# Two gated feed-forward layers: first groups of the second product at even distances, first tiles' taps and SiLU one per step, last roundings and plain products in another order

## The chip, the core and the metric

The kernel runs on one core of a Trainium2 chip. Its engines are PE (TensorE, matrix products), DVE (VectorE), ACT (ScalarE), POOL (GpSimd) and SP (SyncE, which here only issues transfers). Each engine works through its own queue in order, and semaphores join the queues. The metric is the device time of one execution in microseconds; less is better.

## What is computed

A trunk of two layers over 1024 tokens of width 1024: linear attention with a feed-forward block, then banded attention with another. The change lies in the feed-forward block, which runs once per layer:

```python
FFN_DIM = 2816
FFN_CONV = 3
def conv_ffn(xn, w_up, conv_w, conv_b, w_down):
    h = causal_dwconv(xn @ w_up, conv_w) + conv_b
    gate, val = h[..., :FFN_DIM], h[..., FFN_DIM:]
    return (jax.nn.silu(gate) * val) @ w_down
...
        h = h + conv_ffn(rmsnorm(h, f_norm[layer]), f_w_up[layer], f_conv[layer], f_conv_b[layer], f_w_down[layer])
    return rmsnorm(h, final_norm)
```

## The kernel before

All of it is in the function `ffn`, called for layer 0 and for layer 1. The 2816 hidden channels are 22 tiles of 128 (`FP` = 22), numbered j = 0 to 21; each has a gate half and a value half.

*Numbers.* A float32 operand is split into a high part (a rounding on ACT: `uh` for weights of the first product, `dh` and `eh` for the second, `fh` for the last weights) and a low part, the rest (a subtraction on POOL or DVE: `ul`, `dl`, `el`, `fl`). A product of blocks is three matmuls for each of four slices of the inner dimension (`triple`: high × high, low × high, high × low, lines 1454 to 1456), so 12 matmuls of 512 columns.

*First product.* For tile j the block (gate, value) × (first, second half of the tokens) is computed with seven block products instead of eight (n = 1 to 7), which needs sums of the raw weight tiles `r11`, `r12`, `r21`, `r22` (`left_sum`, DVE) and of the inputs (`sums`, once). `operand(j, n)` makes the sum, `uh` (ACT) and `ul` (POOL from step 17's operands on, DVE before); `product(j, n)` runs on PE; `after(j, n)` takes the result out of PSUM: to `keep` (n = 1 on ACT, n = 6 on DVE, where it is two operations), to `gpre` and `vpre`, the gate and value before the convolution.

*Between the products.* `taps(j, v, step)` is the convolution, for value (v = 1) and gate (v = 0): step 0 on ACT, steps 1 and 2 on DVE. Then `silu` on ACT, `gated` (value × gate, DVE), and for tiles 18 to 21 `hidden`, the split into `hidh` (ACT) and `hidl` (DVE).

*Second product.* Tiles 0 to 17 are taken in pairs: nine groups g = 0 to 8 (`NG`), each again seven block products (n in the order 1, 2, 5, 3, 6, 7, 4) with `weights`, `channels` (sums on DVE, splits on ACT, POOL and DVE), `second` (PE), `drain` (the two PSUM banks to `stage`: for n = 6 and 7 two adds on DVE, else two copies on ACT) and `send` (POOL issues two transfers that add `stage` to sums in DRAM). What n = 1 contributes to three further blocks is collected in `d_e`, loaded back at the end by `load_e(u)` and added there by `send_e(u, n)`, also on POOL. Tiles 18 to 21 are multiplied plainly at the very end (`part` in layer 0, `tile_of` in layer 1): their weights come by `load_last` (SP) and are split by `cut_last(q)`, q = 0 to 7. In layer 1 the residual is brought in by `load_r` and `load_t` (SP), with transposes on PE.

*The order.* It is written out by hand. `seq` is the list of PE's steps; `pos` gives a step's number. `at(i, f, rank)` hangs a job before step i, jobs of one step in order of rank:

```python
            for i in range(len(seq) + 8):
                for _, f in sorted(jobs.pop(i, ()), key=lambda j_: j_[0]):
                    f()
                if i < len(seq):
                    seq[i]()
```

So this loop sets each engine's queue. Steps 0 to 7 are the plain products of tile 0; from step 8 on each step is one block product, up to step 217 (`end`); then come the plain products of tiles 18 to 21. The operands of a step are issued two steps ahead with rank 1 (`operand`) or three ahead with rank 1.2 and 1.4 (`weights`, `channels`), `after` and `drain` one step later with rank 0, `send` two later with rank 0.5. Group g's products begin at steps 24, 41, 62, 83 and 104 for g = 0 to 4. From group 1 on, a group's products stand three steps apart, two products of the first kind between them, and two steps lie from one group's last to the next one's first only between groups 0 and 1 (39 to 41). In group 0 they stand at 24, 26, 29, 31, 34, 36 and 39. `fin_at` = 206 is the last product of group 8.

*Buffers that matter.* Four PSUM banks of 512 columns (tag `u`) for the first product and, at the end, for the plain products; two of 1024 (tag `d`) for the second, both used by every block product. `stage` and the value tiles share SBUF tiles.

Of the kernel before, what the change touches and what calls it, by code (L numbers as in the profile page):

```python
# [18 lines left out]
KT = 8  # L19
# [3 lines left out]
FP = 22  # L23
# [5 lines left out]
def trunk_kernel(  # L29
# [26 lines left out]
    o = 0  # L56
# [512 lines left out]
    with ExitStack() as ph:  # L569
# [140 lines left out]
        def heads(t):  # L710

            return t // 2, range(4 * (t % 2), 4 * (t % 2) + 4)
# [633 lines left out]
        ORDER = [(w[0], int(w[1])) for w in "k0 k1 k2 k3 q0 q1 k4 q2 q3 k5 v0 v1 k6 v2 v3 k7 q4 q5 q6 q7 v4 v5 v6 v7".split()]  # L1346
# [17 lines left out]
        with tc.manual_schedule(engines={mybir.EngineType.PE, mybir.EngineType.DVE, mybir.EngineType.Activation}):  # L1364
            tails = []
            acts, normed = [[[[None, None] for _ in range(KT)] for _ in range(2)] for _ in range(2)]
            for t in range(4):
                s, hds = heads(t)
# [47 lines left out]
    def ffn(layer, h, hp, xs, tail, d_r, last):  # L1416
# [19 lines left out]
        def at(i, f, rank=1):  # L1436

            jobs.setdefault(max(i, 0), []).append((rank, f))
# [6 lines left out]
        def cut_low(src, hi, lo, eng):  # L1445
            tt(eng, lo, src, hi.bitcast(F32), sub)
# [58 lines left out]
        def left_sum(j, n):  # L1505
            a = lambda q: raw[j, q]
            if (j, n) in summed:
                return
            summed.add((j, n))
            if n == 7:  # L1510
                tt(nc.vector, a(21), a(11), a(21), sub)
            elif n == 6:
                tt(nc.vector, a(21), a(22), a(21), sub)
            elif n == 5:
                tt(nc.vector, a(11), a(21), a(11), add)
            elif n == 3:
                tt(nc.vector, a(12), a(12), a(21), sub)

        def operand(j, n, lo=True):

            a = lambda q: raw[j, q]
            left_sum(j, n)
            src = a({1: 11, 2: 12, 7: 21, 6: 21, 5: 11, 4: 22, 3: 12}[n])
            ops[j, n] = cut_high(src, "u")
            if lo:
                cut_low(src, *ops[j, n], nc.gpsimd)
            return lambda: cut_low(src, *ops[j, n], nc.vector)
# [69 lines left out]
        pos = {}  # L1597
        ORDER = 1, 2, 5, 3, 6, 7, 4

        def step(key, f):  # L1600
            pos[key] = len(seq)
            seq.append(f)
# [29 lines left out]
        for c, (j, n) in enumerate(plan):  # L1632
            pos[c // 7 + 1, c % 7 + 1] = pos["p", j, n] = len(seq)
            due[len(seq)] = (j, n)
            step((j, -n), lambda j=j, n=n: product(j, n))
            for g in range(NG):
                for n, o in zip(ORDER, (2, 3, 5, 6, 8, 9, 11) if g == 0 else (-2, 0, 2, 4, 6, 8, 10)):
                    if c == 7 * (2 * g + 1) + 6 + o:
                        step(("d", g, n), lambda g=g, n=n: second(g, n))
        end, fin_at = pos[FP - 1, 7], pos["d", NG - 1, 4]  # L1640
        early = pos["p", 1, 3]
        for i, (j, n) in due.items():
            if i < early:
                low = []
                at(i - 2, lambda j=j, n=n, low=low: low.append(operand(j, n, False)), 1)
                at(i - 2, lambda low=low: low[0](), 2.5)
            else:
                at(i - 2, lambda j=j, n=n: operand(j, n), 1)
                if j > 3 and n in (6, 4):
                    at(i - 2, lambda j=j, n=n: left_sum(j, n - 1), 1.05)  # L1650
            if n != 2 or j > 2:
                at(i + 1, lambda j=j, n=n: after(j, n), 0)

        def nx(j, s):
            return pos[j + 1, s] if j + 1 < FP else end + s
# [23 lines left out]
        for j in range(3, FP - 1):  # L1679
# [2 lines left out]

        v0, v1, v2, g0, g1, g2 = [(v, i) for v in (1, 0) for i in range(3)]
        when = {
            0: [(11, (g0,), 0), (12, (v0,), 0), (13, (v1,), 2), (13, (v2,), 2.7), (15, (g1, g2, silu), 2), (17, (gated,), 2)],
            1: [(18, (v0, v1), 2), (19, (v2, g0), 2), (20, (g1,), 2), (21, (g2, silu), 2), (22, (gated,), 2)],
            2: [(24, (v0, v1), 2), (25, (v2, g0), 2), (26, (g1,), 2), (27, (g2, silu), 2), (28, (gated,), 2)],
        }
        for j in range(3, FP - 1):
            when[j] = [(pos[j, 7], (v0, v1), 2), (nx(j, 1), (v2, g0), 2), (nx(j, 2), (g1,), 2)]  # L1690
            when[j] += [(nx(j, 3), (g2,), 2), (nx(j, 4), (silu,), 1.6), (nx(j, 5), (gated,), 2)]
            if j >= 2 * NG:
                when[j].append(({18: fin_at + 5, 19: fin_at + 7}.get(j, nx(j, 6)), (hidden,), 1.9))
        for j, w_ in when.items():
            for i, fs, r in w_:
                at(i, lambda j=j, fs=fs: [taps(j, *f) if isinstance(f, tuple) else f(j) for f in fs], r)
# [99 lines left out]
        def send_e(u, n):  # L1796
            nc.gpsimd.dma_start(out=total(n, u), in_=stage["e", u], accum_op=add)
# [20 lines left out]

        for u, i in ((0, pos["d", NG - 1, 5]), (1, fin_at + 2)):
            at(i, lambda u=u: load_e(u), 3)  # L1820
            for k, n in enumerate((6, 7, 4)):
                at(i + 2 + k // 2, lambda u=u, n=n: send_e(u, n), 0.6)


        k0 = 2 * NG
        fw, fh, fps, norms = {}, {}, {}, []
        n0 = len(seq)
        slots = [(k, 1) for k in range(4)] + [(k, 1) for k in range(4, 8)] if layer == 0 else [(k, 0) for k in range(4)] + [(k, 1) for k in range(4)]
        last_at = [pos[FP - 1, s] for s in (3, 4, 5, 6)] + [end + 1] * 4
        if layer == 1:  # L1830
            last_at = [pos[FP - 1, 2]] + last_at[:-1]
            last_at[5] = end
            last_at[7] = end + 2

        def load_last(q):
            tag = ("a11", "a12", "r11", "r21", "r22", "r11", "r22", "r21")[q]
# [11 lines left out]
        def cut_last(q):  # L1848
            k, s = slots[q]
            hi, lo = [actp.tile([P, HALF], F32R, name=f"f{x}{q}", tag=f"x{x}{k}_{s}") for x in "hl"]  # L1850
            nc.scalar.copy(hi, fw[q])
            cut_low(fw[q], hi, lo, nc.gpsimd if q % 2 else nc.vector)
            fw[q] = hi, lo

        for q in range(8):
            s = (1, 1, 2, 3, 4, 4, 5, 6)[q]
            at(fin_at + 1 if q < 2 else pos[FP - 1, s], lambda q=q: load_last(q), 1)
            at(last_at[q], lambda q=q: cut_last(q), 1.5)

        if layer == 0:  # L1860

            def part(s, m, ks):
                def f():
                    if ks[0] == 0:
                        if s == 0 and m > 3:
                            if m % 2 == 0:
                                fps["d"] = pacc.tile([P, SEQ], F32, name="pf", tag="d", bufs=2)
                            fps[s, m] = fps["d"][:, hs(m % 2)]
                        else:
                            fps[s, m] = pacc.tile([P, HALF], F32, name="pf", tag="u", bufs=4)  # L1870
                    for k in ks:
                        triple(fps[s, m], fw[m], [t_[:, hs(s)] for t_ in hid[k0 + k]], kc[k], k == 0, k == 3)
                        if (s, m, k) in ((1, 5, 1), (1, 6, 0)):
                            next(norms[0])
                return f
# [10 lines left out]
                            next(norms[0], None)  # L1886
                return f

            for m in range(KT):
                step(("f", 0, m, 0), part(0, m, range(3)))  # L1890
            for m in range(KT):
                step(("f", 0, m), part(0, m, range(3, 4)))
            for m in range(KT):
                step(("f", 1, m), part(1, m, range(4)))
            for s in range(2):
# [20 lines left out]
        else:  # L1916
# [19 lines left out]
            def tile_of(t, ks):  # L1936
                def f():
                    if ks[0] == 0:
                        if t in (0, 1, 4, 5):
                            ps = pacc.tile([P, SEQ], F32, name="pf", tag="d", bufs=2)  # L1940
                            fps[t] = [ps[:, hs(c)] for c in range(2)]
                        else:
                            fps[t] = [pacc.tile([P, HALF], F32, name="pf", tag="u", bufs=4) for _ in range(2)]
                    for c in range(2):
                        if ks[0] == 0:
                            for f in range(4):
                                nc.tensor.matmul(fps[t][c][:, f * P : (f + 1) * P], res[t, c][:, f], ident, is_transpose=True, start=f == 0, stop=False, skip_group_check=True)
                        for k in ks:
                            hh, hl = [x_[:, t * P : (t + 1) * P] for x_ in hid[k0 + k]]
                            hi, lo = fw[2 * k + c]  # L1950
                            mm(fps[t][c], hh, hi, start=False, stop=False, skip_group_check=True)
                            mm(fps[t][c], hh, lo, start=False, stop=False, skip_group_check=True)
                            mm(fps[t][c], hl, hi, start=False, stop=k == 3, skip_group_check=True)
                return f
# [17 lines left out]
                        next(its[t], None)  # L1972
                return f

            for t in range(4):
                step(("f", t, 0), tile_of(t, range(3)))
            for t in range(4):
                step(("f", t), tile_of(t, range(3, 4)))
            for t in range(4, KT):
                step(("f", t), tile_of(t, range(4)))  # L1980
            at(end, lambda: last(None, None, fin), 3)
# [418 lines left out]
```

## Time and profile before

| | us |
|---|---|
| median of three runs | 2600.73 (2599.67 to 2603.17) |
| the profiled execution | 2599.32 |
| its span, first to last instruction | 2597.6 |
| PE, DVE, ACT, POOL busy | 2513.0, 1862.1, 1414.8, 1480.1 |
| granted TensorE clock, mean | 0.993 |

One execution was profiled. A row of the timeline gives start, duration, engine, line, operation and tiles, and in brackets how long the engine had been idle and what ended that. A matmul of 512 columns is shown with some 0.39 us, but the next begins about 0.23 us after it: they overlap, so progress is told by their number and starts, not by their busy time. By the starts, layer 0's steps 0 to 217 run from 681.6 to 1299.1 us, layer 1's from 1914.1 to 2539.2.

### The profile page before, as it was taken

How to read it: one execution, taken by the hardware profiler on the slowest of the kernel's cores; microseconds unless marked ns; L12 is line 12 of the kernel's file. 1: busy time of each engine (PE TensorE's matmuls, PEld its weight loads, DVE VectorE, ACT ScalarE, POOL GpSimd, SP SyncE). 2: the span in 40 equal slices, each digit the busy share in tenths (PEclk: the TensorE clock that was granted, in tenths of full speed). 3: DMA queues.
4: the chain of work that ended last, by engine and by line, in shares of the span. 5: the costliest groups of instructions: out<-in, count | busy, mean ns of one | idle time of the engine just before them, and what ended most of it. 6: DMA issues, size and time to landing. Idle time of an engine off the chain costs nothing.

```text
span 2597.6 us, 39406 instructions
## 1 busy us (share of the span) xinstructions
PE 2513.0 (97%) x13933; PEld 2073.2 (80%) x13933; DVE 1862.1 (72%) x3102; ACT 1414.8 (54%) x2735; POOL 1480.1 (57%) x1470
## 2 busy tenths in 40 slices
PE   7999999999999999999999999998999999999998
PEld 5878788888877888888778888887877788888877
DVE  5765764554588888888876666666478788888876
ACT  6444455464455555565455555555445656565643
POOL 3655543345447777777736444443443777777771
PEclk9999999999999999999999999999999999999999
DMA  4534435555436767777841211113232567777785
GB/s 127 139 100 119 124 101 160 146 165 161 115 81 139 149 144 154 155 146 156 180 141 57 61 53 54 51 54 105 89 111 77 134 145 147 147 156 155 155 191 178
DMA packets 319238, 326.20 MB, mean 126 GB/s; under 512 B 32960, under 2 KB 242624, under 8 KB 319040
## 3 DMA queue, kind: packets, MB, share of 16 engines
q1 hardware_dynamic: 287904, 219.59, 28.7%
q0 software_dynamic: 26240, 95.43, 20.6%
q10 hardware_dynamic: 4896, 8.65, 0.9%
q8 instruction: 110, 1.80, 0.3%
q14 instruction: 88, 0.72, 0.1%
HBM read 180.42 MB, written 143.20 MB: 125 GB/s over the span
## 4 chain that ended last, share of the span: by engine, by line
PE 55%; DVE 5%; POOL 3%; issue 3%; ACT 2%; DMA 1%; DVEq 0%; ACTq 0%; POOLq 0%
PE pu L1456 8%; PE pu L1454 8%; PE pu L1455 8%; PE pd L1456 4%; PE pd L1455 4%; PE pd L1454 4%; PE acc L119 3%; PE acc L120 3%; PE acc L121 3%; POOL ul L1421 2%; PE ptp L2134 2%; PE sc L2106 1%; DMA r<-in_f_w_up_dram 1%; PE poT L2164 1%; PE poT L2163 1%
## 5 line engine op out<-in xcount | busy, mean ns | idle before, releaser
L1421 POOL TENSOR_TENSOR ul<-r,uh 128x512 fp32r<-128x512 f32 x282 | 445.8, 1599 | 301.9 <-ACT uh L1442 277.8
L119 PE MATMUL acc<-xh,whi 128*128 128x512 f32 x896 | 377.1, 421 | 0.2 <-ACT xh L1160 0.2
L120 PE MATMUL acc<-xl,whi 128*128 128x512 f32 x896 | 355.1, 396 | 1.6 <-POOL xl L421 1.0
L121 PE MATMUL acc<-xh,wlo 128*128 128x512 f32 x896 | 353.9, 395 | 0.0
L1442 ACT CAST uh<-r 128x512 fp32r<-128x512 f32 x296 | 181.8, 623 | 219.5 <-DVE r L1421 166.6
L104 POOL TENSOR_TENSOR wlo<-wraw,whi 128x256 fp32r<-128x256 f32 (+2 forms) x206 | 169.7, 852 | 165.0 <-ACT whi L102 144.6
L1454 PE MATMUL pu<-xh,uh 128*128 128x512 f32 x552 | 217.0, 393 | 5.2 <-ACT uh L1442 2.0
L1456 PE MATMUL pu<-xh,ul 128*128 128x512 f32 x552 | 216.9, 393 | 4.3 <-POOL ul L1421 4.2
L1455 PE MATMUL pu<-xl,uh 128*128 128x512 f32 x552 | 216.3, 392 | 1.0 <-POOL xl L421 1.0
L1775 ACT COPY stage<-pd 128x1024 f32<-128x1024 f32 x180 | 174.9, 1013 | 49.5 <-PE pd L1456 49.4
L121 PEld LDWEIGHTS acc<-xh,wlo 128*128 128x128 f32 x896 | 169.8, 189 | 37.9
L120 PEld LDWEIGHTS acc<-xl,whi 128*128 128x128 f32 x896 | 171.3, 191 | 24.7 <-POOL xl L421 3.1
L119 PEld LDWEIGHTS acc<-xh,whi 128*128 128x128 f32 x896 | 170.9, 191 | 22.0 <-ACT xh L1160 1.0
L2114 POOL TENSOR_SCALAR sS<-sS,st 128x640 f32<-128x640 f32 (+4 forms) x128 | 85.2, 668 | 172.8 <-DVE st L2113 129.1
L1549 DVE SCALAR_TENSOR_TENSOR val<-vpre,colt,val 128x1023 f32<-128x1023 f32 (+2 forms) x92 | 152.5, 1658 | 38.6 <-ACT val L1546 38.4
L1421 POOL TENSOR_TENSOR dl<-a,dh 128x512 fp32r<-128x512 f32 x90 | 154.7, 1719 | 38.5 <-ACT dh L1442 38.5
L1549 DVE SCALAR_TENSOR_TENSOR gate<-gpre,colt,gate 128x1023 f32<-128x1023 f32 (+2 forms) x92 | 174.9, 1902 | 0.8
L1421 DVE TENSOR_TENSOR r<-r,r 128x512 f32<-128x512 f32 x168 | 131.8, 785 | 31.0 <-POOL ul L1421 29.5
L2112 ACT ACTIVATE sS<-sS,st 128x640 f32<-128x640 f32 (+4 forms) x128 | 89.2, 697 | 102.5 <-DVE st L2111 98.6
L1456 PEld LDWEIGHTS pu<-xh,ul 128*128 128x128 f32 x552 | 104.3, 189 | 29.4 <-POOL ul L1421 7.7
L1454 PEld LDWEIGHTS pu<-xh,uh 128*128 128x128 f32 x552 | 104.3, 189 | 28.1 <-ACT uh L1442 2.4
L1455 PEld LDWEIGHTS pu<-xl,uh 128*128 128x128 f32 x552 | 104.4, 189 | 23.7 <-POOL xl L421 2.1
(401 smaller groups left out, 7163.6 us busy)
## 6 DMA issues: line engine op xcount, KB each, us to landing
r<-in_f_w_up_dram SPq DMA_DIRECT2D x172, 256.0 KB, 4.4
d_r<-stage POOLq DMA_DIRECT2D x78, 512.0 KB, 7.7
d_c<-stage POOLq DMA_DIRECT2D x70, 512.0 KB, 8.1
a<-in_f_w_down_dram SPq DMA_DIRECT2D x72, 256.0 KB, 2.8
wraw<-in_a_w_in_dram SPq DMA_DIRECT2D x32, 512.0 KB, 4.6
d_e<-stage POOLq DMA_DIRECT2D x32, 512.0 KB, 9.0
wraw<-in_a_w_out_dram SPq DMA_DIRECT2D x16, 512.0 KB, 4.2
d_r<-h ACTq DMA_DIRECT2D x32, 256.0 KB, 3.9
```

The lines of the kernel that those rows point to most:

```text
L104: nc.gpsimd.tensor_tensor(lo[:, c], raw[:, c], hi[:, c].bitcast(F32), op=ALU.subtract)
L119: mm(ps, hi[:, kw, wcol : wcol + P], rh[k][s], start=st, stop=False)
L120: mm(ps, hi[:, kw, wcol : wcol + P], rl[k][s], start=False, stop=False)
L121: mm(ps, lo[:, kw, wcol : wcol + P], rh[k][s], start=False, stop=sp)
L1421: tt = lambda eng, o, a, b, op: eng.tensor_tensor(o, a, b, op=op)
L1442: copy(hi, src)
L1454: mm(ps, w[0][:, cw], x[0], start=first, stop=False, skip_group_check=True)
L1455: mm(ps, w[0][:, cw], x[1], start=False, stop=False, skip_group_check=True)
L1456: mm(ps, w[1][:, cw], x[0], start=False, stop=last, skip_group_check=True)
L1549: nc.vector.scalar_tensor_tensor(t_[:, a:c1], p_[:, a - step : c1 - step], w[:, 2 - step : 3 - step], t_[:, a:c1], op0=ALU.mult, op1=ALU.add)
L1775: nc.scalar.copy(t_, ps)
L2112: nc.scalar.activation(S, S, AF.Exp, bias=st[:, 1:2], accum_out=st[:, 2:3])
```

## The change

It moves work between steps; no instruction is added or removed (the same number on each engine).

1. Positions of the second product's groups: group g begins after first product 7(2g + 1) + 6 + max(2 − g, −2) and goes on every second one. Group 0 now stands at steps 24, 27, 30, 33, 36, 39, 42; groups 1 to 3 begin at 44, 64 and 84 (before 41, 62, 83), three steps apart within; from group 4 on all is as before. Two steps lie between groups at 42 to 44, 62 to 64, 82 to 84 and 102 to 104.
2. Tiles 0, 1 and 2: the gate's second and third taps, `silu` and `gated` get steps of their own (before, taps or tap and `silu` shared one).
3. Tile 20: these four a step later. `hidden(19)` from step 213 to 215, `hidden(20)` from 216 to 218. The sum for (21, 7) a step earlier.
4. `send_e`: two of three (u = 0) or all three (u = 1) behind the step's operands, the later ones a step later.
5. `cut_last`: other steps, and in layer 0 an earlier rank.
6. The plain products of the first eight (layer 0) or four (layer 1) blocks in three passes (tiles 18 and 19, then 20, then 21) instead of two (18 to 20, then 21).

```diff
-                for n, o in zip(ORDER, (2, 3, 5, 6, 8, 9, 11) if g == 0 else (-2, 0, 2, 4, 6, 8, 10)):
-                    if c == 7 * (2 * g + 1) + 6 + o:
+                for i, n in enumerate(ORDER):
+                    if c == 7 * (2 * g + 1) + 6 + max(2 - g, -2) + 2 * i:
                         step(("d", g, n), lambda g=g, n=n: second(g, n))
...
                 at(i - 2, lambda j=j, n=n: operand(j, n), 1)
+                if j == FP - 1 and n == 1:
+                    at(i - 2, lambda j=j: left_sum(j, 7), 1.05)
...
-            0: [(11, (g0,), 0), (12, (v0,), 0), (13, (v1,), 2), (13, (v2,), 2.7), (15, (g1, g2, silu), 2), (17, (gated,), 2)],
-            1: [(18, (v0, v1), 2), (19, (v2, g0), 2), (20, (g1,), 2), (21, (g2, silu), 2), (22, (gated,), 2)],
-            2: [(24, (v0, v1), 2), (25, (v2, g0), 2), (26, (g1,), 2), (27, (g2, silu), 2), (28, (gated,), 2)],
+            0: [(11, (g0,), 0), (12, (v0,), 0), (13, (v1,), 2), (13, (v2,), 2.7), (15, (g1,), 2), (16, (g2,), 2), (17, (silu,), 1.6), (18, (gated,), 2)],
+            1: [(18, (v0, v1), 2), (19, (v2, g0), 2), (20, (g1,), 2), (21, (g2,), 2), (22, (silu,), 1.6), (23, (gated,), 2)],
+            2: [(24, (v0, v1), 2), (25, (v2, g0), 2), (26, (g1,), 2), (27, (g2,), 2), (28, (silu,), 1.6), (29, (gated,), 2)],
         }
         for j in range(3, FP - 1):
-            when[j] = [(pos[j, 7], (v0, v1), 2), (nx(j, 1), (v2, g0), 2), (nx(j, 2), (g1,), 2)]
-            when[j] += [(nx(j, 3), (g2,), 2), (nx(j, 4), (silu,), 1.6), (nx(j, 5), (gated,), 2)]
+            late_ = 1 if j == FP - 2 else 0
+            when[j] = [(pos[j, 7], (v0, v1), 2), (nx(j, 1), (v2, g0), 2), (nx(j, 2 + late_), (g1,), 2)]
+            when[j] += [(nx(j, 3 + late_), (g2,), 2), (nx(j, 4 + late_), (silu,), 1.6), (nx(j, 5 + late_), (gated,), 2)]
             if j >= 2 * NG:
-                when[j].append(({18: fin_at + 5, 19: fin_at + 7}.get(j, nx(j, 6)), (hidden,), 1.9))
+                when[j].append(({18: fin_at + 5, 19: pos[FP - 1, 5], 20: end + 1}[j], (hidden,), 1.9))
...
             at(i, lambda u=u: load_e(u), 3)
-            for k, n in enumerate((6, 7, 4)):
-                at(i + 2 + k // 2, lambda u=u, n=n: send_e(u, n), 0.6)
+            for n, (k, r) in zip((6, 7, 4), ((2, 0.6), (2, 2.9), (3, 2.9)) if u == 0 else ((2, 2.9), (3, 2.9), (4, 2.9))):
+                at(i + k, lambda u=u, n=n: send_e(u, n), r)
...
-        last_at = [pos[FP - 1, s] for s in (3, 4, 5, 6)] + [end + 1] * 4
-        if layer == 1:
-            last_at = [pos[FP - 1, 2]] + last_at[:-1]
-            last_at[5] = end
-            last_at[7] = end + 2
+        last_at = [pos[FP - 1, s] for s in (3, 4, 5, 6)] + ([end, end, end + 1, end + 1], [end + 1, end + 1, end + 3, end + 3])[layer]
...
-            at(last_at[q], lambda q=q: cut_last(q), 1.5)
+            at(last_at[q], lambda q=q: cut_last(q), 0.9 if layer == 0 else 1.5)
...
-            for m in range(KT):
-                step(("f", 0, m, 0), part(0, m, range(3)))
-            for m in range(KT):
-                step(("f", 0, m), part(0, m, range(3, 4)))
+            for i, ks in enumerate((range(2), range(2, 3), range(3, 4))):
+                for m in range(KT):
+                    step(("f", 0, m, i) if i < 2 else ("f", 0, m), part(0, m, ks))
```

The last edit is made likewise for `tile_of` in layer 1, over four blocks.

More of the change, by code (lines that the diff above doesn't have):

```diff
@@ L1973, in closing @@
                 return f
[L1975 to L1978, printed above, removed]
+            for i, ks in enumerate((range(2), range(2, 3), range(3, 4))):
+                for t in range(4):
+                    step(("f", t, i) if i < 2 else ("f", t), tile_of(t, ks))
             for t in range(4, KT):
```

## The prediction

> **What bounds the kernel now.** I read the page's span, busy shares and chain of waits first, then the windows (busy time by stretch, its edges put on step starts), then the timeline of each engine where a window comes out too long.
>
> ```profile
> span 2597.6 us, 39406 instructions
> PE 2513.0 (97%) x13933; PEld 2073.2 (80%) x13933; DVE 1862.1 (72%) x3102; ACT 1414.8 (54%) x2735; POOL 1480.1 (57%) x1470
> PE 55%; DVE 5%; POOL 3%; issue 3%; ACT 2%; DMA 1%; DVEq 0%; ACTq 0%; POOLq 0%
> ```
>
> TensorE sets the end, and the change leaves it every matmul. So the only thing to win is time in which PE stands still inside the two FFNs. How much that is, the windows tell; the columns are stretch, length, then busy time and instruction count of PE, PEld, DVE, ACT, POOL, then PE clock, DMA share and GB/s.
>
> ```profile
> 728.00:809.50 81.50, 75.25 (x313) 57.38 (x313) 68.75 (x65) 44.61 (x63) 49.34 (x37) 1.00 0.45 103
> 809.50:1225.30 415.80, 415.48 (x1825) 341.79 (x1824) 350.80 (x326) 246.94 (x349) 322.69 (x241) 1.00 0.73 150
> 1225.30:1249.00 23.70, 22.68 (x97) 17.79 (x96) 20.87 (x19) 12.87 (x19) 18.49 (x15) 1.00 0.73 145
> 1281.60:1299.10 17.50, 14.11 (x50) 10.80 (x49) 15.64 (x12) 6.19 (x9) 9.51 (x6) 0.80 0.64 179
> 1968.70:2046.10 77.40, 71.65 (x301) 55.31 (x301) 64.05 (x65) 43.10 (x60) 43.74 (x28) 1.00 0.35 117
> 2464.30:2487.80 23.50, 22.66 (x97) 17.70 (x96) 20.86 (x19) 12.88 (x19) 18.32 (x15) 1.00 0.74 135
> 2517.80:2539.20 21.40, 16.17 (x61) 11.49 (x60) 17.08 (x14) 10.11 (x16) 11.29 (x8) 0.92 0.96 252
> ```
>
> The second row is the FFN at its pace: 1824 matmuls (152 steps of 12) in 415.8 us, 0.228 us a matmul, 2.735 us a step. (One matmul more in a count is the neighbour that overlaps the edge.) Priced so, the other rows hold too much time: steps 16 to 41 of layer 0 (312 matmuls) 81.5 − 71.1 = 10.4 us; steps 194 to 201 (96) 23.7 − 21.9 = 1.8; steps 214 to 217 (48) 17.5 − 10.9 = 6.6. Layer 1: steps 16 to 40 (300) 77.4 − 68.4 = 9.0; 194 to 201 1.6; 213 to 217 (60) 21.4 − 13.7 = 7.7. Together 37.1 us: the most that this change can win, and its edits lie on just these places.
>
> **Part 1: first groups at even distances, taps and SiLU one per step.** Waits at steps 17, 18 and 25 show the mechanism.
>
> ```profile
> 731.97 0.50 PE L1456 MATMUL pu<-xh,ul 128*128 128x512 f32 x1 [0.52 <-POOL ul L1421]
> 737.12 0.50 PE L1456 MATMUL pu<-xt2h,ul 128*128 128x512 f32 x1 [1.73 <-POOL ul L1421]
> 757.78 0.50 PE L1456 MATMUL pu<-xt2h,ul 128*128 128x512 f32 x1 [0.62 <-POOL ul L1421]
> 729.50 3.50 DVE L1549 SCALAR_TENSOR_TENSOR gate<-gpre,colt,gate 128x1023 f32<-128x1023 f32 x2
> 732.92 0.68 DVE L1421 TENSOR_TENSOR r<-r,r 128x512 f32<-128x512 f32 x1
> 733.03 1.06 ACT L1552 ACTIVATE gate<-gate 128x1024 f32<-128x1024 f32 x1 [1.42 <-DVE gate L1549]
> 734.00 0.60 ACT L1442 CAST uh<-r 128x512 fp32r<-128x512 f32 x1
> 753.29 1.23 DVE L1421 TENSOR_TENSOR val<-val,gate 128x1024 f32<-128x1024 f32 x1 [1.19 <-ACT gate L1552]
> 755.04 0.68 DVE L1421 TENSOR_TENSOR r<-r,r 128x512 f32<-128x512 f32 x1
> ```
>
> PE waits for a low part `ul`; that waits for the high part `uh`; that for a sum `r` on DVE, which stands behind work of no hurry. At step 18 it is two taps in one go (3.50 us), and `uh` then also stands behind the SiLU. With one tap at step 15 and the other after the sum, `r` comes 1.75 us earlier, and the SiLU a step later no longer precedes `uh` (1.06 us): 2.8 us against a stall of 2.0, which goes. At step 25 the product `gated` waits 1.19 us for its SiLU and runs 1.23, all ahead of `r`; it moves behind `r`: 2.4 us against some 1.5. For tile 2 the same separation keeps an `uh` from standing behind a SiLU that waits for taps (step 30 of before).
>
> The rest of the stretch is plain overload, and that is what the positions of the groups change.
>
> ```profile
> L1421 DVE TENSOR_TENSOR r<-r,r x168: 674/691/3917, 711.8 to 2533.4; 128x512 f32<-128x512 f32 x168
> L1421 DVE TENSOR_TENSOR stage<-pd,stage x72: 1206/1210/1225, 788.7 to 2497.9; 128x1024 f32<-128x1024 f32 x72
> L1421 DVE TENSOR_TENSOR r<-r,r 128x512 f32<-128x512 f32 x168 | 131.8, 785 | 31.0 <-POOL ul L1421 29.5
> L1549 DVE SCALAR_TENSOR_TENSOR gate<-gpre,colt,gate 128x1023 f32<-128x1023 f32 (+2 forms) x92 | 174.9, 1902 | 0.8
> L1421 DVE TENSOR_TENSOR val<-val,gate 128x1024 f32<-128x1024 f32 x42 | 70.5, 1678 | 2.4 <-ACT gate L1552 2.4
> ```
>
> (The first two give minimum/median/maximum in ns, the others mean ns.) Before, steps 33 to 38 issue to DVE 11 operations of 512 columns (0.75 us, between the median and the mean of `r`), 3 taps (1.8, a little under the mean here) and 4 adds to `stage` (1.21): 18.5 us due in 6 × 2.735 = 16.4. After it, the heaviest six steps there (36 to 41) have 10, one tap, one `gated` (1.7, the last row) and 4 adds: 15.8. Steps 26 to 28 had 12.0 us due in 8.2; their successors 26 to 29 have 10.5 in 10.9. So the backlog that makes `ul` and `el` late no longer builds up. I keep the wait at step 17 (its sum stands ahead of both taps, so nothing changes for it; 0.52 us idle, 0.8 with the restart) and 1.0 for what remains: gain 10.4 − 1.8 = 8.6 in layer 0, 9.0 − 1.8 = 7.2 in layer 1.
>
> What it costs: between the last product of a group and the first of the next there is now one step, not two, at all four turns from group 0 to group 4 (before, at one). In it ACT must drain both banks.
>
> ```profile
> 804.10 1.91 ACT L1775 COPY stage<-pd 128x1024 f32<-128x1024 f32 x2
> 806.79 0.39 PE L1454 MATMUL pd<-eh,dh 128*128 128x512 f32 x1
> 1242.97 0.51 PE L1454 MATMUL pd<-eh,dh 128*128 128x512 f32 x1 [0.81 <-ACT stage L1775]
> ```
>
> The one such turn of before cost nothing, with 0.8 us to spare; where the drain stood behind a late cast (third row) it cost 0.81. Between 0 and 0.8 I take 0.3, for three new turns a layer: 0.9. A stall here makes PE late, and gives ACT and DVE that time. Part 1 is worth 15.8 − 1.8 = **14.0 us** (bounds: 19.4 if all goes; 7 if half the waits come back).
>
> **Part 2: the end of layer 0.** Order on DVE, and what PE does meanwhile:
>
> ```profile
> 1284.95 2.31 DVE L1421 TENSOR_TENSOR hidl<-val,hidh 128x1024 fp32r<-128x1024 f32 x1
> 1287.19 2.28 DVE L1549 SCALAR_TENSOR_TENSOR gate<-gpre,colt,gate 128x1022 f32<-128x1022 f32 x1
> 1289.40 1.41 DVE L1421 TENSOR_TENSOR keep<-pu,keep 128x512 f32<-128x512 f32 x2
> 1290.95 0.77 PE L1454 MATMUL pu<-xt4h,uh 128*128 128x512 f32 x1 [3.36 <-DVE keep L1421]
> 1291.94 0.63 PE L1456 MATMUL pu<-xt4h,ul 128*128 128x512 f32 x1
> 1292.37 0.63 PE L1454 MATMUL pu<-xt4h,uh 128*128 128x512 f32 x1
> ```
>
> `hidl` of tile 19 and the second gate tap of tile 20 (4.6 us) now come behind `keep`. What stands ahead of them is the same in both, so `keep` can run at 1284.95 and end at 1286.4, before PE wants it at 1287.4. The wait goes, and with it the slow stretch behind it (0.43 us from matmul to matmul). What is late next: the plain products now begin 6.5 us earlier, and the fourth of them takes the PSUM bank that `gpre` of the last tile (DVE) must have read. From 1284.95 to the end of that `gpre` DVE has 11 operations of 512 columns (0.68) and 3 of 1024 (1.21; up to 2.3 as in the rows here): 11.1 to 14.4 us, 1296.1 to 1299.4. PE arrives there at 1299.1 − 6.5 + 18 × 0.228 = 1296.7. Between nothing and 2.7 I take 1.6: gain **5.0** of 6.6 (bounds 3 and 6.6). Splitting the plain products in three passes adds no matmul and no weight load, and defers tile 20 by 48 matmuls × 0.228 = 10.9 us, so its moved `hidden` has cover.
>
> By the Trainium skill (TensorE: Matmul & The Clock Gate, "What's actually happening") the clock halves after an idle window of about 3.4 us and a matmul of 512 columns then takes 426.7 ns; the 0.43 here agrees. By that rule a rest of 1.6 us would cost only itself; the rows of layer 1 (clock 0.92, no wait above 2.2 us) say that two shorter waits close together can slow PE too.
>
> **Part 3: the end of layer 1.** Here the first cause is a transfer.
>
> ```profile
> 2525.63 0.62 ACT L1442 CAST uh<-r 128x512 fp32r<-128x512 f32 x1 [5.71 <-DMA r<-in_f_w_up_dram]
> 2533.63 0.48 PE L1454 MATMUL pu<-xt4h,uh 128*128 128x512 f32 x1 [2.22 <-DVE keep L1421]
> 2527.75 2.18 DVE L1421 TENSOR_TENSOR hidl<-val,hidh 128x1024 fp32r<-128x1024 f32 x1 [4.29 <-ACT hidh L1566]
> 2532.07 1.41 DVE L1421 TENSOR_TENSOR keep<-pu,keep 128x512 f32<-128x512 f32 x2
> r<-in_f_w_up_dram SPq DMA_DIRECT2D x1, 256.0 KB, 16.8
> q0 software_dynamic: 992, 3.60, 42.8%
> 2516.09 0.87 POOL L1797 DMA_DIRECT2D d_c<-stage x1 [2.77 <-DMA d_c<-stage]
> ```
>
> (The rows of `r` and q0: transfers issued from 2500 to 2545; this `r` needs 16.8 us to land.) ACT waits for it, `hidh` and so `hidl` wait behind ACT, and `keep` behind `hidl`. The change takes `hidl` out of that line, so the second wait (2.2 us, with a slow clock) goes. The transfer itself it only helps: three adds of `stage` into DRAM move 1 to 2 steps later and behind POOL's subtractions. Seven of them took 42.8% of 40 us of all DMA engines, 2.45 us each; two that no longer compete before the landing let `r` land about 2 us earlier (between 0 and their 4.9; less than half, as the queues share). POOL's wait of 2.77 us ahead of a subtraction goes too. But `fh0` now stands behind that cast, and DVE behind `fh0`, so a rest of 2.7 us stays: gain **5.0** of 7.7 (bounds 2 and 7.7).
>
> **Part 4: steps 194 to 201.** Two of three adds move behind the subtractions, 0.87 us of POOL each: 0.5 us a layer, **1.0** (bounds 0 and 3.4). The sum of `r` for the last tile, a step earlier, and the roundings in another order cost nothing: the same instructions, hidden behind PE, which would show 0.7 us each where that cover is gone.
>
> **Sum.** 14.0 + 5.0 + 5.0 + 1.0 = 25.0 us. The profiled execution took 2599.32 us (1.7 around its span), so 2574.3; the median of the runs is 1.4 above it: 2600.73 − 25.0 = **2576 us**.
>
> **Rivals.** (a) *The waits come back one by one.* PE that arrives earlier meets the next late operand, since DVE and POOL have as much work as before. For it: in the long window DVE and POOL are busy 84% and 78%, and `r` stretches up to 3.9 us. Against it: that window, with the same work per step, holds PE at 2.735. Price: part 1 brings 5, the ends 5 together, part 4 nothing: 2591.
>
> The Trainium skill (SBUF — State Buffer, "SBUF: two separate sides") has DVE and GpSimd exclude each other for whole instructions where DVE has two SBUF inputs; `r` (two SBUF inputs) stretches and `stage` (one from PSUM, 1206 to 1225) does not, which agrees. By that rule rival (a) gains weight; the full PE of the long window limits it.
>
> (b) *Slower: the drains at the turns.* If at the six new turns ACT's two copies stand behind a cast whose sum is late by more than 3 us, PE waits as at 1290.95 and restarts slowly: 6.4 us a turn, 38 us, against 25 gained: 2614. It decides from 4.2 us a turn. Against it: 0 and 0.81 are what such places cost in the trace.
>
> (c) *The ends stay as they are* (DVE's work bounds the last tile, the order doesn't matter), part 1 holds: 2600.7 − 14 = 2587. Against it: PE waits for `keep`, which the new order frees.
>
> (d) *Nothing is left of the stalls*: 2600.7 − 37.1 = 2564.
>
> **Chances.** My forecast (2570 to 2582) 0.48; (a) 0.20; (c) 0.13; (d) 0.09; no change, where gains and new waits cancel, 0.05; (b) 0.05. Leaving out (b), no change and the far end of (a): 2563 to 2593. A difference of 0.2% (5.2 us) is about what a measurement of this kernel can tell. Faster 0.88, within 0.2% 0.06, slower 0.06.
>
> **What would show it.** Right: the windows over steps 16 to 41 near 73 and 71 us, no PE wait for `keep` at step 216 in either layer, no SiLU idle ahead of a `uh` in the first tiles, `r` landing under 16 us. Wrong: PE waits for `ACT stage` at steps 44, 64, 84 and 104 (b), new waits for `ul` between steps 42 and 110 (a), a wait of some us at the fourth plain product (part 2), ACT still waiting 5 us for `r` (part 3).

## The result, and the profile after

The changed kernel is slower: 2617.75 us (median of 4 runs, 2616.1 to 2621.45) against 2600.91 (2599.67 to 2603.17), ratio 1.0071 (95% interval 1.0057 to 1.0085), +16.8 us where −25 was predicted. Span, busy time and chain of waits after:

```profile
span 2616.5 us, 39341 instructions
PE 2517.9 (96%) x13933; PEld 2074.8 (79%) x13933; DVE 1880.0 (72%) x3102; ACT 1413.6 (54%) x2735; POOL 1463.1 (56%) x1470
PE 57%; DVE 11%; issue 7%; POOL 7%; ACT 4%; DMA 3%; SPq 0%; DVEq 0%; POOLq 0%; ACTq 0%
```

DVE has the same 3102 instructions and is busy 17.9 us longer (1880.0 − 1862.1), so some of them became longer. Its share of the chain went from 5% to 11%.

The windows of the changed kernel, edges on step starts (columns as in the prediction): layer 0's steps 16 to 41, 42 to 103, 214 to 217 and its plain products, then layer 1's 16 to 40, 41 to 103 and 213 to 217.

```profile
728.60:811.40 82.80, 75.85 (x314) 60.15 (x314) 67.48 (x65) 42.80 (x61) 48.34 (x33) 0.96 0.37 91
811.40:993.70 182.30, 174.91 (x746) 139.45 (x744) 151.75 (x136) 101.15 (x143) 128.91 (x100) 0.99 0.70 141
1295.90:1308.00 12.10, 11.18 (x50) 8.94 (x49) 11.71 (x9) 5.63 (x9) 6.34 (x6) 1.00 0.77 195
1308.00:1359.70 51.70, 47.85 (x210) 38.85 (x208) 38.17 (x50) 28.08 (x57) 12.53 (x9) 0.97 0.54 183
1982.30:2061.70 79.40, 71.96 (x302) 56.57 (x302) 64.77 (x64) 42.71 (x61) 44.58 (x29) 0.98 0.27 90
2061.70:2243.00 181.30, 176.23 (x758) 142.02 (x757) 152.26 (x137) 101.36 (x143) 125.53 (x97) 0.99 0.68 145
2542.70:2558.10 15.40, 13.80 (x61) 11.13 (x60) 12.89 (x11) 6.63 (x11) 8.59 (x7) 1.00 1.08 297
```

The stretches that the prediction did not show, in the kernel before: steps 42 to 103 of layer 0, 41 to 103 of layer 1, the plain products of layer 0.

```profile
809.50:979.10 169.60, 169.45 (x745) 139.40 (x744) 144.20 (x134) 100.23 (x142) 132.31 (x100) 1.00 0.72 149
2046.10:2218.00 171.90, 171.78 (x757) 141.72 (x757) 141.30 (x133) 101.50 (x144) 133.34 (x100) 1.00 0.69 143
1299.10:1345.80 46.70, 45.66 (x210) 37.75 (x208) 33.30 (x48) 27.65 (x57) 11.41 (x8) 1.00 0.55 188
```

After minus before, stretch by stretch (the rows between are made the same way):

| stretch | layer 0 | layer 1 | predicted, both |
|---|---|---|---|
| steps 16 to 41 (40) | +1.3 | +2.0 | −15.8 |
| to step 103 | +12.7 | +9.4 | +1.8 |
| 104 to 193 | −0.7 | −0.7 | 0 |
| 194 to 201 | −0.8 | −0.8 | −1.0 |
| 202 to 213 (212) | +1.2 | +1.5 | 0 |
| to 217 | −5.4 | −6.0 | −11.6 |
| plain products | +5.0 | 0.0 | +1.6 |

The sum, +18.7, is the difference of the spans (18.9) but for 0.2 us. So the ends did most of what was said, layer 0's gave it back at once, and the loss lies where the prediction looked for almost nothing: groups 1 to 3.

The main waits of PE in the changed kernel's layer 0, from its timeline: steps 20, 34, 82 and 216 (layer 1 has these too) and the fourth plain product. The one at step 216 is what is left of the 3.36 us of before.

```profile
744.02 0.76 PE L1454 MATMUL pu<-xt4h,uh 128*128 128x512 f32 x1 [3.25 <-DVE keep L1421]
785.85 0.50 PE L1454 MATMUL pu<-x7h,uh 128*128 128x512 f32 x1 [1.08 <-ACT uh L1442]
931.31 0.77 PE L1454 MATMUL pd<-eh,dh 128*128 128x512 f32 x1 [2.83 <-ACT dh L1442]
931.87 0.63 PE L1455 MATMUL pd<-el,dh 128*128 128x512 f32 x1
932.30 0.63 PE L1456 MATMUL pd<-eh,dl 128*128 128x512 f32 x1
1302.45 0.47 PE L1454 MATMUL pu<-xt4h,uh 128*128 128x512 f32 x1 [0.92 <-DVE keep L1421]
1314.18 0.47 PE L1454 MATMUL pf<-hidh,fh 128*128 128x512 f32 x1 [1.95 <-DVE gpre L1421]
```

Behind 744.02 and 931.31 the matmuls start 0.43 us apart for a while, so each costs nearly 5 us (in layer 1 step 20 goes on at 0.23 us at once and costs 3.4). Who is late at 931.31 (step 82, the last product of group 2) is read from the other engines' timelines: DVE, POOL, ACT.

```profile
919.92 6.80 DVE L1549 SCALAR_TENSOR_TENSOR gate<-gpre,colt,gate 128x1023 f32<-128x1023 f32 x2
926.65 1.40 DVE L1421 TENSOR_TENSOR keep<-pu,keep 128x512 f32<-128x512 f32 x2
927.97 0.68 DVE L1421 TENSOR_TENSOR val<-val 128x512 f32<-128x512 f32 x1
921.24 3.15 POOL L1421 TENSOR_TENSOR ul<-r,uh 128x512 fp32r<-128x512 f32 x2
923.74 1.89 POOL L1421 TENSOR_TENSOR dl<-a,dh 128x512 fp32r<-128x512 f32 x1
928.68 0.62 ACT L1442 CAST eh<-val 128x512 fp32r<-128x512 f32 x1 [8.73 <-DVE val L1421]
```

Two gate taps take 6.80 us, 1.3 for the first and 5.5 for the second, which ends 1.1 us after POOL's third subtraction in a row. Behind it stands the value sum that the product needs; ACT waits 8.73 us for it with `eh`; behind `eh` in ACT's queue stand a SiLU and a `uh`, and then the `dh` that PE waits for. The kernel before has the same long pair beside the same three, and PE loses nothing:

```profile
908.84 0.68 DVE L1421 TENSOR_TENSOR val<-val 128x512 f32<-128x512 f32 x1
913.42 6.12 DVE L1549 SCALAR_TENSOR_TENSOR gate<-gpre,colt,gate 128x1023 f32<-128x1023 f32 x2
919.47 1.41 DVE L1421 TENSOR_TENSOR keep<-pu,keep 128x512 f32<-128x512 f32 x2
920.79 0.68 DVE L1421 TENSOR_TENSOR el<-val,eh 128x512 fp32r<-128x512 f32 x1
914.37 2.85 POOL L1421 TENSOR_TENSOR ul<-r,uh 128x512 fp32r<-128x512 f32 x2
917.06 1.39 POOL L1421 TENSOR_TENSOR dl<-a,dh 128x512 fp32r<-128x512 f32 x1
```

There the sum for the group's last product was made before the taps (first row), and behind them stands nothing but `keep` and a low part for the next group, both in time. The new position puts the sum behind them. This wait, with its slow restart, is 4.7 us of the +12.7 in layer 0 and 4.6 of the +9.4 in layer 1. Of the rest, 6.8 and 3.2 us are lost by step 70, in waits for `ul`, `el` and `stage` of at most 0.83 us each; what makes those late was not followed one by one.

### The profile page after: what moved, and what is told of

The parts are those of the page before. It is cut to its first block, busy times and chain, and to the rows that moved or that the text cites. A ratio compares the mean times of both kernels' runs of the same rounds, so it can differ in the third digit from the quotient of the medians.

```text
span 2616.5 us, 39341 instructions
## 1 busy us (share of the span) xinstructions
PE 2517.9 (96%) x13933; PEld 2074.8 (79%) x13933; DVE 1880.0 (72%) x3102; ACT 1413.6 (54%) x2735; POOL 1463.1 (56%) x1470
## 4 chain that ended last, share of the span: by engine, by line
PE 57%; DVE 11%; issue 7%; POOL 7%; ACT 4%; DMA 3%; SPq 0%; DVEq 0%; POOLq 0%; ACTq 0%
PE pu L1456 7%; PE pu L1454 7%; PE pu L1455 7%; PE acc L119 4%; PE acc L120 4%; PE acc L121 4%; POOL ul L1421 3%; PE pd L1456 3%; PE pd L1454 3%; PE pd L1455 3%; PE acco L119 2%; PE acco L120 2%; PE acco L121 2%; PE ptp L2131 2%; POOL dl L1421 1%
## 5 line engine op out<-in xcount | busy, mean ns | idle before, releaser
L1421 DVE TENSOR_TENSOR r<-r,r 128x512 f32<-128x512 f32 x168 | 153.4, 913 | 32.5 <-POOL ul L1421 31.0
L1549 DVE SCALAR_TENSOR_TENSOR val<-vpre,colt,val 128x1023 f32<-128x1023 f32 (+2 forms) x92 | 135.5, 1473 | 53.2 <-ACT val L1546 52.9
L1421 DVE TENSOR_TENSOR el<-val,eh 128x512 fp32r<-128x512 f32 x90 | 102.2, 1135 | 44.8 <-ACT eh L1442 44.8
```

Source lines behind the costliest of these rows:

```text
L1421: tt = lambda eng, o, a, b, op: eng.tensor_tensor(o, a, b, op=op)
L1549: nc.vector.scalar_tensor_tensor(t_[:, a:c1], p_[:, a - step : c1 - step], w[:, 2 - step : 3 - step], t_[:, a:c1], op0=ALU.mult, op1=ALU.add)
```

## The experiments

All times are against the kernel before on the same chip.

| run | median us | ratio (95%) | difference |
|---|---|---|---|
| the change | 2617.75 | 1.0071 (1.0057 to 1.0085) | +16.8 |
| e1 positions alone | 2623.87 | 1.0088 (1.0073 to 1.0103) | +24.2 |
| e2 taps alone | 2602.39 | 1.0011 (1.0002 to 1.0021) | +2.7 |
| e3 ends alone | 2592.95 | 0.9973 (0.9961 to 0.9984) | −6.8 |
| e4 all but positions | 2594.03 | 0.9976 (0.9967 to 0.9986) | −5.7 |
| e5 groups 1, 2 at +0 | 2625.67 | 1.0110 (1.0093 to 1.0126) | +27.3 |
| e6 groups 1 to 3 at −1 | 2600.47 | 1.0006 (0.9997 to 1.0015) | +2.1 |
| e7 one tap later | 2616.01 | 1.0071 (1.0056 to 1.0087) | +17.7 |
| e8 two `ul` on DVE | 2615.51 | 1.0066 (1.0051 to 1.0081) | +17.2 |
| e9 ends, `gpre` first | 2592.20 | 0.9968 (0.9956 to 0.9980) | −7.7 |
| e10 e9, two `ul` on DVE | 2590.38 | 0.9960 (0.9947 to 0.9972) | −9.5 |
| e11 tile 0 as before | 2613.63 | 1.0052 (1.0038 to 1.0066) | +13.8 |
| e12 28 `ul` on DVE | 2612.30 | 1.0048 (1.0032 to 1.0065) | +12.5 |

**Which edit: e1 to e4.** The kernel before with edit 1 of the change (e1), edit 2 (e2), edits 3 to 6 (e3), edits 2 to 6 (e4). In e2 and e4 the value for group 0's second product is split at step 23 before `gated(1)` of that step, so the product uses it before its gating. The instructions are the same, but this split does not wait for `gated(1)`, so these two leave out a wait that the right sums would need.

```diff
-                for n, o in zip(ORDER, (2, 3, 5, 6, 8, 9, 11) if g == 0 else (-2, 0, 2, 4, 6, 8, 10)):
-                    if c == 7 * (2 * g + 1) + 6 + o:
+                for i, n in enumerate(ORDER):
+                    if c == 7 * (2 * g + 1) + 6 + max(2 - g, -2) + 2 * i:
```

> The kernel before with the new positions of the second product's groups alone. Theory P (the loss is the positions: groups 0 to 3 now fall on other first products than the groups from 4 on, so their sums, splits and drains coincide with the taps and the DVE and POOL queues run late): by the starts of PE's steps in the trace of the change, steps 31 to 104 lose about 15 us in layer 0 and 12.5 in layer 1, so +24 to +28 us against before. Theory T (the taps and SiLU one step later make the first tiles' values late, and the groups inherit the lateness): the positions by themselves still save what the prediction gave them, -5 to -14 us.

> The kernel before with the first tiles' taps, SiLU and gated edit alone. Theory P: PE's wait for keep at step 20 (3.3 us idle and a slow clock after it) about cancels the waits of steps 18 and 25 that go, so -3 to +1 us. Theory T: +10 us or more.

> The kernel before with the edits of the last tiles alone (tile 20 and hidden later, the early sum, send_e, the roundings, three passes). Theory E1 (as the trace of the change has it: layer 1's end gains 5.9 us, layer 0's keep wait gains 5 and the plain products give that back to gpre, h and nacc, the middle gains 0.8 us a layer): -6 to -8 us. Theory E2 (layer 0's plain products were late only because everything before them was): -10 to -12 us, as predicted.

> The changed kernel with the groups back at the positions of before. Theory P: -7 to -11 us against before, that is 24 to 28 under the changed kernel. Theory T: still slower than before, +5 us or more.

The positions cost +24.2, as theory P has it, and the change without them is 5.7 us faster than before, a little less than P's 7: theory T falls. The taps alone cost 2.7, above P's +1. The three parts add to 20.1 (24.2 + 2.7 − 6.8) and the change measures 16.8, so they are not quite independent: alone, each of e1 and e2 has in both layers a wait for ACT's `stage` in group 0 (in layer 0 2.40 us at step 30 and 2.89 at step 31) that the change does not have. E1 holds: in e3 the ends bring 6.8, not 10. The wait for `keep` at step 20 is in the change, e2 and e4 (3.2 us), and not in e1 and e3, so it belongs to the taps.

**Why the positions: e5 and e6.** Group 0 as before, groups 1 to 3 shifted.

```diff
-                for n, o in zip(ORDER, (2, 3, 5, 6, 8, 9, 11) if g == 0 else (-2, 0, 2, 4, 6, 8, 10)):
+                for n, o in zip(ORDER, (2, 3, 5, 6, 8, 9, 11) if g == 0 else [((0 if g < 3 else -1) if g < 4 else -2) + 2 * i for i in range(7)]):
```

(e6 has −1 for groups 1, 2 and 3.)

> The kernel before with groups 1 and 2 two first products later (their products behind the same first products of the tile as group 2 of the change), group 3 one later; group 0 as before, so no turn of two steps before group 3. Theory Phase (the price lies in which first products a group stands behind, and is paid anew by each group): by the trace of the change a group at this place loses 7.3 us in layer 0 and 6.6 in layer 1, group 3's place 0.5, so 2 x 13.9 + 1 = about +29 us against before. Theory Turns (the loss is the backlog that the two-step turns leave, handed on from group 0): two turns of two steps a layer remain, +10 us at most.

> The kernel before with groups 1, 2 and 3 one first product later; group 0 as before. Theory Phase: the place of group 3 in the change, 0.5 us a group and layer, so +3 us against before (and none of the waits for dh or stage that groups 1 and 2 of the change show). Theory Turns: one turn of two steps a layer, +2 to +5 us: this run alone does not tell them apart, the pair does.

+27.3 us decides for theory Phase; e6's +2.1 (its interval includes no change) fits both, as was said before it ran. In e5 the long waits, as PE's list of waits over groups 1 to 3 of layer 0 has them (total us, times, longest):

```profile
PE pd L1454 <- ACT gpre L1591: 2.8, 1, 2.8
PE pd L1454 <- ACT dh L1442: 2.8, 1, 2.8
```

They stand at steps 61 and 82, the last products of groups 1 and 2, in both layers alike. At step 61 it is the chain of above again: two gate taps of 6.80 us ahead of the value sum, ACT's `eh` waiting 8.74 us for that sum, and ACT's next instructions behind it. So the price is paid anew by each group at this place, without a turn of two steps or a late group 0 ahead of it. e6 has neither wait.

**What is late: e7, e8 and e12.** e7 puts tile 7's second gate tap behind the value sum; e8 makes two of the three low parts ahead of it on DVE; e12 all low parts of tiles 5 to 8. Each is the changed kernel with one of these:

```diff
-            when[j] += [(nx(j, 3 + late_), (g2,), 2), (nx(j, 4 + late_), (silu,), 1.6), (nx(j, 5 + late_), (gated,), 2)]
+            when[j] += [(nx(j, 3 + late_) + (j == 7), (g2,), 2), (nx(j, 4 + late_), (silu,), 1.6), (nx(j, 5 + late_), (gated,), 2)]
...
-                cut_low(src, *ops[j, n], nc.gpsimd)
+                cut_low(src, *ops[j, n], nc.vector if (j, n) in ((8, 5), (8, 2)) else nc.gpsimd)
...
+                cut_low(src, *ops[j, n], nc.vector if j in (5, 6, 7, 8) else nc.gpsimd)
```

> The changed kernel with one instruction a layer moved: the second gate tap of tile 7 from step 78 to 79, behind keep and the value sum for the last product of group 2. Theory Order (PE's wait of 2.8 us for dh at step 82 comes from that tap, 5.5 us long, standing ahead of the value sum on DVE): the wait and the slow matmuls behind it go, 4.7 us a layer, so -7 to -9.5 us against the changed kernel, +8 to +10 against before. Theory Overload (DVE and POOL are late there in any order): the wait stays or moves, 0 to -3 us against the changed kernel, +14 to +17 against before.

> The changed kernel with two of tile 8's low parts (ul of its fourth and fifth product) made on DVE, not POOL. Theory Shared access (the tap took 5.5 us and not 1.3 because DVE stood still while POOL ran ul, ul and dl back to back): DVE has 1.4 us more to do and yet is earlier, the tap falls to some 2.5 us or less, the wait for dh at step 82 goes or falls under 1 us; -4 to -9 us against the changed kernel. Theory Overload (DVE has too much to do): DVE gets 1.4 us more, so the wait at step 82 grows to some 4 us; +2 to +4 against the changed kernel, +19 to +21 against before.

> The changed kernel with all low parts ul of tiles 5 to 8 (28 a layer) on DVE, not POOL: that is the stretch from step 42 to 84 in which the change loses most. DVE gets 28 x 0.69 = 19 us more to do there, POOL loses 28 x 1.6. Theory Shared access (the loss there is DVE standing still beside POOL's runs of subtractions): the stretched sums, taps and products get back to 0.7 and 1.3 us, which is worth more than 19 us of DVE, and steps 42 to 104 take 174 us or less (182.4 in the change, 169.6 before); -8 us or more against the changed kernel. Theory Overload (DVE has too much to do at these places, the stretching only adds to it): PE waits for ul and keep from DVE, steps 42 to 104 take 185 us or more; +5 us or more against the changed kernel.

e7's total is Overload's, no gain; but its rows show the wait nearly halved and moved. At the place of the stretched tap (DVE, ACT and PE):

```profile
921.29 3.72 DVE L1421 TENSOR_TENSOR val<-val 128x512 f32<-128x512 f32 x1
926.31 1.28 DVE L1549 SCALAR_TENSOR_TENSOR gate<-gpre,colt,gate 128x1022 f32<-128x1022 f32 x1
927.68 1.06 ACT L1552 ACTIVATE gate<-gate 128x1024 f32<-128x1024 f32 x1 [2.01 <-DVE gate L1549]
928.87 0.47 PE L1454 MATMUL pd<-eh,dh 128*128 128x512 f32 x1 [1.56 <-ACT gate L1552]
```

The tap is 1.28 us now and the value sum 3.72 instead of 0.68: the next instruction with both inputs in SBUF stands until POOL is through. The SiLU then waits for the tap ahead of `dh`, and the wait is 1.56 for 2.83. By step starts 2.5 us are won here by step 84 in layer 0 and 2.4 in layer 1. Layer 0 keeps 1.3 of them to step 104; layer 1 loses them and 1.4 more by step 92, at `uh` and `ul` of step 88 (1.0 and 0.9 us), waits that the changed kernel does not have. In e8 DVE has more to do and is earlier:

```profile
918.69 1.31 DVE L1549 SCALAR_TENSOR_TENSOR gate<-gpre,colt,gate 128x1023 f32<-128x1023 f32 x1
919.91 2.56 DVE L1421 TENSOR_TENSOR ul<-r,uh 128x512 fp32r<-128x512 f32 x1
922.40 1.27 DVE L1549 SCALAR_TENSOR_TENSOR gate<-gpre,colt,gate 128x1022 f32<-128x1022 f32 x1
923.59 1.40 DVE L1421 TENSOR_TENSOR keep<-pu,keep 128x512 f32<-128x512 f32 x2
928.85 0.47 PE L1454 MATMUL pd<-eh,dh 128*128 128x512 f32 x1 [0.60 <-ACT dh L1442]
```

Both taps take 1.3 us and the wait is 0.60: theory Shared access at this place; Overload would have made it 4. The total (+17.2) is neither theory's: the kernel gains nothing certain, with the same waits as in e7 at layer 1's step 88. e12's steps 42 to 103 of layer 0:

```profile
809.65:989.37 179.72, 172.97 (x745) 138.44 (x744) 150.37 (x164) 101.23 (x143) 85.51 (x72) 1.00 0.70 143
```

28 instructions more on DVE (19 us by 0.69) and no more busy time (150.4 for 151.8 in the change), so the time that DVE stood still was worth as much as they are. But the stretch keeps 179.7 us, between the two forecasts: what bunches at these positions stays late with the one engine or the other. How the remaining 10 us (against 169.6) divide among its small waits for `ul`, `el`, `stage` and `dh` (none above 1.0 us) stays open.

**The taps: e11.** The changed kernel with tile 0 back.

```diff
-            0: [(11, (g0,), 0), (12, (v0,), 0), (13, (v1,), 2), (13, (v2,), 2.7), (15, (g1,), 2), (16, (g2,), 2), (17, (silu,), 1.6), (18, (gated,), 2)],
+            0: [(11, (g0,), 0), (12, (v0,), 0), (13, (v1,), 2), (13, (v2,), 2.7), (15, (g1, g2, silu), 2), (17, (gated,), 2)],
```

> The changed kernel with tile 0's taps, SiLU and gated as before (tiles 1 and 2 as changed). Theory Tile 0 (PE's wait of 3.3 us for keep at step 20 comes from its SiLU, a step later and now ahead of the casts and the first tap of tile 1's value on ACT): that wait and its slow matmuls go (5.1 us a layer), the stall of step 18 comes back (2 us a layer), so -4 to -7 us against the changed kernel, +10 to +13 against before. Theory Positions (the wait at step 20 has to do with the groups): it stays; +17 against before.

+13.8 for +16.8, a little under the forecast's gain, which had counted a slow restart in both layers. The intervals touch, but the trace is plain: no wait at step 20 in either layer. How the SiLU makes it, in the changed kernel (ACT, then DVE):

```profile
736.72 1.28 ACT L1552 ACT_TABLE_LOAD   x1
738.01 1.06 ACT L1552 ACTIVATE gate<-gate 128x1024 f32<-128x1024 f32 x1
739.96 1.24 ACT L1546 ACTIVATE val<-vpre,colt 128x1024 f32<-128x1024 f32 x1
741.24 1.31 DVE L1549 SCALAR_TENSOR_TENSOR val<-vpre,colt,val 128x1023 f32<-128x1023 f32 x1 [0.91 <-ACT val L1546]
742.47 1.41 DVE L1421 TENSOR_TENSOR keep<-pu,keep 128x512 f32<-128x512 f32 x2
```

It no longer precedes `uh` of step 18, but it precedes tile 1's value on ACT; DVE's tap waits for that, and `keep` stands behind the tap. Ahead of this SiLU ACT also loads a table (first row, 1.28 us). The kernel before has the same load at 730.33, but there it lay in the time in which ACT waited for the taps anyway; now its 1.28 us stand in the line too.

**The ends: e9 and e10.** e3 with tile 21's first taps behind the last `gpre` in layer 0 (e9), and also two of its low parts on DVE (e10).

```diff
-        at(end, half(0, HALF)[0], 2)
+        at(end + 1 - layer, half(0, HALF)[0], (0.5, 2)[layer])
...
-                cut_low(src, *ops[j, n], nc.gpsimd)
+                cut_low(src, *ops[j, n], nc.vector if j == FP - 1 and n in (2, 4) else nc.gpsimd)
```

> The edits of the last tiles alone (as e3), and in layer 0 the first half of tile 21's taps behind the last gpre. Theory Rest (layer 0's plain products stand still 2 us for gpre because three taps, 2.3 us, precede it on DVE, and the slow matmuls behind it cost 1.8 more): that wait goes, the plain products take 3 to 4 us less, so -9.5 to -11 us against before (e3: -6.8). Theory Norm (DVE's chain of nacc sums sets when layer 0 ends, whatever PE does): PE waits that much longer at the sums of the norm, nothing is won, -6 to -7.5.

> As e9, and the low parts of (21, 2) and (21, 4) on DVE, not POOL, in both layers. Theory Shared access (keep is late at step 216, 0.9 and 1.6 us, since the DVE instruction ahead of it, 5.2 and 4.4 us long, stood still while POOL ran three subtractions back to back): with one left in a row keep is 1.5 us or more earlier though DVE has 1.4 us more ahead of it, both waits go, -2.5 to -3.5 us against e9. Theory Overload: keep is 1.4 us later, +2 to +4 us against e9.

In e9 the wait for `gpre` goes and another comes in the same plain products, for the sum `h` that frees a PSUM bank:

```profile
1331.02 0.79 PE L1454 MATMUL pf<-hidh,fh 128*128 128x512 f32 x1 [2.87 <-DVE h L1421]
1337.74 1.05 PE L412 MATMUL pss<-ones,nacc 128*128 128x2 f32 x8 [0.77 <-DVE nacc L409]
1319.32 2.47 DVE L401 TENSOR_TENSOR nacc<-nacc,nt 128x512 f32<-128x512 f32 x1 [4.19 <-ACT nt L399]
```

So 0.9 us where theory Rest had 3 to 4, near theory Norm: the line of `h` and `nacc` sums sets layer 0's end. It is not DVE's alone: the third row shows DVE waiting 4.19 us for ACT's square `nt` (1.66 at this place before), and ACT makes it behind scalings of the next weights, for whose transfer it waited 2.23 us. e1 says the same without any edit at the end: there the last steps of layer 0 take 2.6 us less than before (the same wait for `keep`, no slow restart), and the plain products 2.7 more. In e10 PE has no wait for `keep` at step 216 in either layer (Shared access); the total is 1.8 us under e9, less than the forecast and with overlapping intervals: layer 0's part ends in the same waits for `h` and `nacc` (2.98 and 1.61 us). e10 is the fastest kernel measured here, 9.5 us under the kernel before.

## Why the prediction was wrong

*Part 1, the positions* failed, and with it the sign. The sum for group 0 took DVE's durations as given and compared 18.5 us with 15.8; the new order has its own late places (step 34: `uh` 1.08, then `ul` 0.90), and steps 16 to 41 came out 1.3 and 2.0 us longer (with the positions alone, e1, 2.9 and 1.4). The larger fault is the sentence on what it costs: only the four turns were looked at. Groups 1 and 2 moved by three and two first products, and none of their sums was laid beside the tile's taps; that stretch ran at full pace, and was taken to stay so. Where 1.8 us were put down for the turns, it cost 22 us (12.7 + 9.4; e1, the positions alone, 12.7 + 9.3). e1, e5 and e6 show the positions to be the cause. How they act is shown for the wait at step 82 (9.3 of the 22 us: a value sum behind a stretched tap, e7 and e8); for the small waits before it the cause stays open.

*Part 1, the taps.* The waits at steps 18 and 25 went as said. That the SiLU "no longer precedes `uh`" was right; what stands behind it on ACT next was not asked, and that made step 20.

*Part 2.* The order of `keep` was right: 5.4 us gained to step 217 (some 2.5 of the 6.6 that the prediction found there was the slow restart, which e1 does not have behind the same wait). A rest of 0.92 stayed, since the tap ahead was stretched beside three POOL subtractions (5.22 us in e3, 2.31 before); the wait for `gpre`, estimated 1.6, is 1.95. The step that failed is that what is won at step 217 is won at the end of the layer: the plain products end where the `h` and `nacc` sums let them (+5.0).

*Part 3* held: 6.0 for 5.0. The rows of `r`, from DMA issues around the changed kernel's end (16.8 us before):

```profile
r<-in_f_w_up_dram SPq DMA_DIRECT2D x1, 256.0 KB, 10.8
```

It needs 6 us less to land, not 2, and ACT waits 1.53 us for it, not 5.71 (whether the moved adds did that was not tested; the prediction's 2.45 us an add came from 40 us, but its row covers 45, so 2.75 by the same count); some 1.5 us were lost again just ahead, in steps 202 to 212. *Part 4*: 1.6 for 1.0.

*The rivals.* None gave the number. (a) had the right engine: what the Trainium skill (SBUF — State Buffer, "SBUF: two separate sides") says of the access that DVE and GpSimd share spoke for it, and the full PE of the long window was taken against it. That window showed only that one arrangement has its stretched instructions where nobody waits. (b), the only one on the slower side, came within 4 us (2614 for 2617.75) by luck: it named the turns and ACT's copies, and no turn of the change waits for them. PE does lose some 5 us to a wait with its slow restart, but at the last product of a group, for a cast behind a late sum. (c) was right on the end of layer 0, wrong on that of layer 1 and on part 1.

## What to carry to other kernels

DVE was 85% busy behind a full PE here, and what kept PE full was an arrangement that fits, not spare time. When a block of work is shifted against another, lay every instruction of both side by side at the new distance, and ask of each long one what stands behind it and when that is wanted. Here three groups shifted by one product cost some 2 us (e6), and two of them shifted by two with the third by one 27 (e5). A wait removed ahead of a serial tail (`h`, `nacc`) is worth what the tail leaves of it.

## What the hardware showed unexpectedly

DVE stood still through a run of POOL instructions, not one: 5.5 us for a tap of 1.3 beside three subtractions, 3.72 for a sum of 0.68 that came in the middle of such a run (e7). Instructions with a PSUM source did not, though 50 of the 84 below ran beside such a subtraction; two lines of the changed kernel (minimum, median, maximum in ns):

```profile
L1421 DVE TENSOR_TENSOR keep<-pu,keep x84: 676/691/694, 727.0 to 2551.8; 128x512 f32<-128x512 f32 x84
L1421 DVE TENSOR_TENSOR el<-val,eh x90: 677/1011/4623, 751.6 to 2520.7; 128x512 fp32r<-128x512 f32 x90
```

And the length of a wait alone does not decide whether PE restarts slowly. At the fourth plain product the changed kernel waits 1.95 us and goes on with 0.23 to 0.30 us a matmul; e3 waits 1.96 at the same place and needs 0.43 (rows of e3):

```profile
1299.89 0.65 PE L1454 MATMUL pf<-hidh,fh 128*128 128x512 f32 x1 [1.96 <-DVE gpre L1421]
1300.34 0.63 PE L1455 MATMUL pf<-hidl,fh 128*128 128x512 f32 x1
1300.77 0.63 PE L1456 MATMUL pf<-hidh,fl 128*128 128x512 f32 x1
```

The same holds at two other places. Step 216 waits 3.36 us in the kernel before and goes on with 0.43, 3.34 in e1 and goes on with 0.23. In the plain products e9's wait of 2.87 restarts slowly, e10's of 2.98 at once at 0.23. The Trainium skill (TensorE: Matmul & The Clock Gate, "What's actually happening") has the clock watched in a window that runs freely; that a wait's place in it decides would fit these rows but is not shown by them, and a slow restart after 1.96 us is earlier than the idle window of some 3.4 us that it names.
